# Graph attention on one core: five sums ahead of the last gather, the result between two one-hots

## The chip, the cores and the metric

The kernel runs on one core of a Trainium2 chip, in one launch. The metric is the device time of an execution in microseconds (us). The core's engines work side by side and meet at semaphores: PE (TensorE, matmuls into PSUM), DVE (VectorE), ACT (ScalarE), POOL (GpSimd) and SP, which here only issues DMAs. Each engine takes its own instructions strictly in the order in which the program gives them.

## The reference

A graph attention layer over 4096 nodes with 64 features, 50000 edges and 4 heads of 64 outputs.

```python
x_proj[h] = x @ weight[h]
for h in range(n_heads):
    src_att = np.sum(x_proj[h, src_nodes] * att_src[h], axis=-1)
    dst_att = np.sum(x_proj[h, dst_nodes] * att_dst[h], axis=-1)
    edge_scores[h] = src_att + dst_att
edge_scores = np.where(edge_scores > 0, edge_scores, 0.2 * edge_scores)
output[h, dst] = sum over its edges of exp(edge_scores[h, i]) * x_proj[h, src]
output[h, dst] /= sum over its edges of exp(edge_scores[h, i]) + 1e-8
```

The last two lines are written here as sums; the reference loops over edges and nodes. The output is node by node, the four heads side by side: 4096 x 256.

## The kernel before

Until about 104 us the edges are sorted: keyed by stretches of source nodes and blocks of destination nodes, sorted on DVE, written out and read back by their counts. Beside it PE computes the scores of all nodes. The result of this stage is, for each of 32 blocks of 128 destination nodes (`b`), a list of edges in 16 groups of 128 places (`NT` = 16), in DRAM (`bin_dram`).

Then a loop over the blocks (`Blocks.run`) does the layer itself. It is software-pipelined by hand: in the turn of block `b`, DVE and PE work on several blocks at once, and the order in which the Python code issues the instructions is the order on each engine. The steps of a turn:

- `load(b + 4)`: SP brings the list of a later block, the same for all partitions, into `bc` (1 MB, one of four buffers).
- `values(b)`: DVE multiplies the gathered features of block `b` by its weights, head by head, into `val`: one instruction over 16 groups x 4 heads x 64 features. The text calls it the product; its line is L641.
- `gather(b + 1, c)` for the three parts `CH` = 6, 6 and 4 groups: PE multiplies one-hot matrices `oh` by the features and scores of the nodes (`xa`, `adb`, L607 to L609) into a PSUM tile `ps` of three banks. There are two such tiles, taken in turn. ACT then takes exponentials of the scores, plain and times 0.2 (`ex`, L619), and copies the gathered one-hots and features into `xs` (L621).
- `project(b - 2)`: PE multiplies the transposed sums `aT` of an earlier block by the weight matrix into the lower half of `pt` (L784); it stands between the second and the third part of the gather.
- `give(b - 2)`: DVE divides that by the denominators (`inv`) into `res` (L794), one of two buffers, and SP stores it to the output (L798).
- `onehot(b + 2)`: DVE compares the list with the partition numbers: two instructions, L589 and L590, the second for the other half of the sources.
- `invert(b - 1)`: reciprocal of denominators, L791. Here some blocks also have one small step of the list `checks`, which counts whether any stretch of edges was too long.
- `weights(b + 1)`: DVE takes the maximum of the two exponentials, L632, into the places of `val` between the features; this makes the leaky ReLU.
- `sums(b)`: PE adds up the 16 groups in one PSUM bank, `acc` (L703), features and denominators together. After groups 9 and 12 it also transposes the two halves of the earlier block's sums into the upper half of `pt` (`turn(b - 1, ...)`, L774); after the second half ACT copies the transposes to `aT` (L779). At the end ACT takes the sums and denominators out of the bank (`take`, L764 and L766).

In one block, `told`, the first of the sums is followed by a matmul with one column that adds up the lengths' flag `long`, in the same bank behind the sums, and DVE compares it into `over` (L706, L707). If it is set, a branch after the loop does everything again in pieces; with these inputs it isn't taken.

The blocks 30 and 31 are computed in another way, with the product in three parts (`lastly`, `last`), and `finish` writes the last result. In three blocks POOL and DVE unpack another window of lists (`unpack`, after the sums).

`pt` is one PSUM bank, `acc` another, the two `ps` tiles take the other six.

Of the kernel before, what the change touches and what calls it, by code (L numbers as in the profile page):

```python
# [11 lines left out]
P = 128  # L12
ALPHA = 0.2
F32 = mybir.dt.float32
BF16 = mybir.dt.bfloat16
I32 = mybir.dt.int32
OP = mybir.AluOpType
# [33 lines left out]
def kernel(ctx: ExitStack, tc: tile.TileContext, x: bass.AP, edge_index: bass.AP,  # L51
# [4 lines left out]
    H, _, Dout = weight.shape  # L56
# [453 lines left out]
    NT = NR  # L510
# [21 lines left out]

    CH = ((0, 6), (6, 6), (12, 4))
    S0 = P + H
    XW = 208
    PW = 256

    class Blocks:
# [39 lines left out]

        def onehot(self, b, t0=0, nt=NT):
            if b >= ND:  # L580
                return
            narrow = self.narrow and b > 0
            if t0 == 0:
                self.oh[b] = self.narrow[b % 2] if narrow else (self.wp if self.narrow else self.bp).tile(
                    [P, 3 * NT * W2], BF16, name="oh")
            oh, bc = self.oh[b], self.bc[b]
            lo, hi = (LOW, HIGH) if narrow else (W2, 0)
            e = (2 * t0 * W2, [2 * W2, nt], [1, W2 + lo])
            V.tensor_scalar(out=av(oh[:], *e), in0=av(bc[:], *e), scalar1=pF[:, 0:1], scalar2=None, op0=OP.is_equal)  # L589
            V.tensor_scalar(out=av(oh[:], (2 * NT + t0) * W2 + hi, [W2, nt], [1, W2 - hi]),  # L590
                            in0=av(bc[:], (2 * t0 + 1) * W2 + hi, [2 * W2, nt], [1, W2 - hi]),
                            scalar1=pF[:, 1:2], scalar2=None, op0=OP.is_equal)

        def gather(self, b, c):

# [20 lines left out]
            for i in range(n):  # L616
                kinds[2](i, t0 + i, start=False, stop=True, skip_group_check=True)
            for k, scale in enumerate((1.0, ALPHA)):
                S.activation(out=av(ex[:], 2 * (k * H * NT + t0), [2, n], [2 * NT, H], [1, 2]),  # L619
                             in_=av(ps[:], P, [PW, n], [1, H], [0, 2]), func=ACTF.Exp, scale=scale)  # L620
# [73 lines left out]

        def sums(self, b, t0=0, n=NT, told=False, between={}):

# [5 lines left out]
            for t in range(t0, t0 + n):  # L702
                T.matmul(out=acc[:, 0:AW], lhsT=xs[:, t, 0:P], rhs=val[:, t, :], start=(t == 0), stop=(t == NT - 1),  # L703
                         **how)
                if t == 0 and told:
                    T.matmul(out=acc[0:1, AW:AW + 1], lhsT=long[:], rhs=ones[:], start=False, stop=True, **how)  # L706
                    V.tensor_scalar(out=over[:], in0=acc[0:1, AW:AW + 1], scalar1=0.5, scalar2=None, op0=OP.is_gt)  # L707
                if t in between:
# [11 lines left out]
        def run(self, first=0, also={}, checks=()):  # L720
# [3 lines left out]
            for b in range(first, ND):  # L724
# [5 lines left out]
                if b not in self.full:  # L730
                    self.values(b)
                for c in range(len(CH)):
                    if c == 2:
                        self.sink.project(b - 2)
                    self.gather(b + 1, c)
                self.sink.give(b - 2)
                self.onehot(b + 2)
                if checks:
                    checks.pop(0)()
                self.sink.invert(b - 1)  # L740
                if apart:
                    self.lastly(b + 1, 0)
                else:
                    self.weights(b + 1)
                self.sums(b, told=b == told, between={9: lambda: self.sink.turn(b - 1, 0), 12: lambda: self.sink.turn(b - 1, 1)})
                if apart:
# [5 lines left out]
    class Finish:  # L752
# [48 lines left out]
        def give(self, b):  # L801
            if b not in self.aT:
                return
            self.aT.pop(b)
            res = self.fp.tile([P, H, Dout], F32, name="res")
            self.scaled(b, res, self.pt[:, 0:C], 0, H)
# [12 lines left out]
        def finish(self, b, to, wait):  # L819
            self.invert(b)  # L820
            res = self.fp.tile([P, H, Dout], F32, name="res")
            for k, t in enumerate(self.aT.pop(b)):
# [230 lines left out]
```

## Time and profile before

| | us |
|---|---|
| median of three runs (277.97 to 278.76) | 278.16 |
| the profiled execution | 278.39 |
| its span, first to last instruction | 276.5 |
| busy in the span: DVE | 246.2 (89%) |
| PE matmuls | 208.8 (75%) |
| PE weight loads | 181.3 (66%) |
| ACT | 202.8 (73%) |
| POOL | 44.4 (16%) |

The span includes the sort, in which DVE is busy and PE mostly not; in the loop over the blocks, 124 to 265 us, DVE, PE and ACT are all busy over nine tenths of the time. The shares alone don't tell which of the three sets the time there: that is read from one block in the timeline, by who stands still, for whom, and for how long. A row of the timeline gives the start, the duration, and in brackets the time for which the engine stood idle just before, with the instruction that released it. Instructions of one engine overlap at their ends, so a step's cost is the distance between starts, not its duration.

### The profile page before, as it was taken

Reading aid. Unit: us, or ns where it says so; the run is one execution under the profiler, and the core shown is the slowest. Engines: PE = TensorE matmul, PEld = TensorE weight load, DVE = VectorE, ACT = ScalarE, POOL = GpSimd, SP = SyncE. Lnnn points to the kernel's source line nnn. Section 1 sums busy time; section 2 is a strip of 40 time slices with the busy share of each in tenths; the row PEclk is TensorE's granted clock in tenths of the full one; section 3 lists DMA queues with packets and bytes.
Section 4 is the critical chain, followed back from the end, with each engine's and each line's share of the span. In section 5 each row is a group of like instructions: output and inputs, shape, how many; then the busy total and the mean of one; then the engine's idle time right before and its main releaser. Section 6 shows DMA issues by size and latency. Waiting matters only on the chain. (4 is left out here: it accounts for less than half of the span.)

```text
span 276.5 us, 6793 instructions
## 1 busy us (share of the span) xinstructions
PE 208.8 (75%) x2551; PEld 181.3 (66%) x2551; DVE 246.2 (89%) x657; ACT 202.8 (73%) x516; POOL 44.4 (16%) x84
## 2 busy tenths in 40 slices
PE   0002769996001998979999999988999999999994
PEld 0002559996001454768888888977888888888883
DVE  4999999919999998889999999997999999998972
ACT  3980650006999929798989898897898989989871
POOL 7898600041000004203030020000000000000000
PEclk9999985555555699999999999999999999999998
DMA  3008000010000001795949558855866757572101
GB/s 116 1 0 163 10 2 2 0 57 19 1 0 0 2 0 47 190 411 165 398 115 385 206 188 342 287 210 193 264 232 233 261 216 293 210 247 111 41 21 63
DMA packets 13190, 39.43 MB, mean 143 GB/s; under 512 B 2208, under 2 KB 8416, under 8 KB 9568
## 3 DMA queue, kind: packets, MB, share of 16 engines
q1 hardware_dynamic: 10752, 36.84, 36.9%
q10 hardware_dynamic: 1696, 1.51, 2.4%
q0 software_dynamic: 704, 0.59, 0.9%
q8 instruction: 21, 0.34, 0.5%
q14 instruction: 17, 0.14, 0.2%
HBM read 33.96 MB, written 4.98 MB: 141 GB/s over the span
## 5 line engine op out<-in xcount | busy, mean ns | idle before, releaser
L621 ACT CAST xs<-ps 128x1176 bf16<-128x1176 f32 (+1 forms) x96 | 103.1, 1076 | 0.0
L641 DVE TENSOR_TENSOR val<-xs,val 128x4096 bf16<-128x4096 bf16 (+2 forms) x35 | 71.7, 2048 | 3.3
L703 PE MATMUL acc<-val,xs 128*128 128x264 bf16 x496 | 67.9, 276 | 1.4 <-DVE over L707 1.3
L607 PE MATMUL ps<-xa,oh 128*128 128x68 bf16 x512 | 51.8, 193 | 9.3 <-ACT xs L621 8.8
L703 PEld LDWEIGHTS <-xs 128*128 128x128 bf16 x496 | 46.5, 98 | 6.8 <-issue 1.5
L608 PEld LDWEIGHTS <-oh 128*128 128x128 bf16 x512 | 40.8, 97 | 15.2 <-issue 15.0
L608 PE MATMUL ps<-adb,oh 128*128 128x132 bf16 x512 | 49.5, 221 | 0.0
L607 PEld LDWEIGHTS <-oh 128*128 128x128 bf16 x512 | 43.9, 98 | 1.0 <-DVE oh L589 0.3
L619 ACT ACTIVATE ex<-ps 128x48 bf16<-128x48 f32 (+1 forms) x192 | 32.8, 243 | 6.7 <-PE ps L608 6.1
L589 DVE TENSOR_SCALAR oh<-bc,pF 128x3328 bf16<-128x3328 bf16 (+4 forms) x38 | 36.0, 948 | 1.8 <-ACT bc L577 1.1
L609 PE MATMUL ps<-xa,oh 128*128 128x68 bf16 x512 | 36.3, 194 | 0.3 <-DVE oh L590 0.3
L609 PEld LDWEIGHTS <-oh 128*128 128x128 bf16 x512 | 28.7, 97 | 0.9 <-DVE oh L590 0.5
L506 PEld LDWEIGHTS scores<-uv,xT 64*128 64x128 f32 x128 | 27.4, 328 | 0.2 <-issue 0.2
L506 PE MATMUL scores<-uv,xT 64*128 64x4 f32 x128 | 27.4, 351 | 0.0
L332 ACT ACTIVATE junk<-kr,nb 128x512 f32<-128x512 f32 x32 | 23.1, 722 | 1.1
L248 DVE TENSOR_TENSOR sB<-sA 128x128 f32<-128x128 f32 (+6 forms) x90 | 22.7, 305 | 0.1
L590 DVE TENSOR_SCALAR oh<-bc,pF 128x1664 bf16<-128x1664 bf16 (+4 forms) x38 | 22.1, 582 | 0.0
L248 DVE TENSOR_TENSOR sZ<-sB 128x128 f32<-128x128 f32 (+7 forms) x87 | 21.7, 302 | 0.1
L794 DVE TENSOR_TENSOR res<-pt,inv 128x256 f32<-128x256 f32 x31 | 13.1, 424 | 9.5 <-PE pt L784 7.5
L784 PE MATMUL pt<-Wbd,aT 128*128 128x128 f32 x124 | 21.4, 295 | 0.1
L779 ACT COPY aT<-pt 128x256 f32<-128x256 f32 x31 | 11.5, 373 | 10.8 <-PE pt L774 10.8
L342 PE MATMUL cnt_ps<-sgn,sel 128*128 128x17 f32 (+1 forms) x10 | 2.2, 349 | 22.9 <-POOL attbd L475 22.9
(173 smaller groups left out, 294.4 us busy)
## 6 DMA issues: line engine op xcount, KB each, us to landing
bc<-gat_bins SPq DMA_DIRECT2D x28, 1024.0 KB, 5.9
out_dram<-res SPq DMA_DIRECT2D x32, 128.0 KB, 2.4
bc<-gat_bins SPq DMA_DIRECT2D x4, 384.0 KB, 4.6
bc<-gat_bins SPq DMA_DIRECT2D x2, 256.0 KB, 5.7
eD<-in_edge_index_dram ACTq DMA_DIRECT2D x2, 195.0 KB, 3.5
eS<-in_edge_index_dram SPq DMA_DIRECT2D x2, 195.0 KB, 3.5
gat_sorted<-sY SPq DMA_DIRECT2D x1, 256.0 KB, 2.0
gat_sorted<-ki SPq DMA_DIRECT2D x1, 256.0 KB, 2.0
```

What stands on the lines that cost most here:

```text
L248: V.tensor_tensor(out=out, in0=in0, in1=in1, op=op)
L332: todo = [lambda b=b: S.activation(out=junk[:], in_=v, func=ACTF.Sign, bias=nbnd[:, b:b + 1], scale=1.0, accum_out=sgn[:, b:b + 1]) for b ...
L506: T.matmul(out=scores[:, k * NB + b, :], lhsT=nodes(b), rhs=uv[:, k, :], start=(k == 0 and b == 0), stop=True, skip_group_check=True)
L589: V.tensor_scalar(out=av(oh[:], *e), in0=av(bc[:], *e), scalar1=pF[:, 0:1], scalar2=None, op0=OP.is_equal)
L590: V.tensor_scalar(out=av(oh[:], (2 * NT + t0) * W2 + hi, [W2, nt], [1, W2 - hi]), in0=av(bc[:], (2 * t0 + 1) * W2 + hi, [2 * W2, nt], [1, ...
L607: kinds = [lambda i, t, **how: T.matmul(out=ps[:, i, P:P + XC], lhsT=hot(2 * t + 1), rhs=xa[:, 2 * t, :], **how), lambda i, t, **how: T.ma ...
L608: lambda i, t, **how: T.matmul(out=ps[:, i, 0:S0], lhsT=hot(2 * t), rhs=adb[:, b, :], **how),
L609: lambda i, t, **how: T.matmul(out=ps[:, i, P:P + XC], lhsT=hot(2 * NT + t), rhs=xa[:, 2 * t + 1, :], **how)]
L619: S.activation(out=av(ex[:], 2 * (k * H * NT + t0), [2, n], [2 * NT, H], [1, 2]), in_=av(ps[:], P, [PW, n], [1, H], [0, 2]), func=ACTF.Exp ...
L621: S.copy(out=xs[:, t0:t0 + n, 0:P + XC], in_=ps[:, 0:n, 0:P + XC])
L641: V.tensor_tensor(out=av(val, t0 * AW, [VW, H * n], [1, Din]), in0=av(xs, S0 + t0 * XW, [XW, n], [0, H], [1, Din]), in1=av(val, t0 * AW + ...
L703: T.matmul(out=acc[:, 0:AW], lhsT=xs[:, t, 0:P], rhs=val[:, t, :], start=(t == 0), stop=(t == NT - 1), **how)
```

## The change

- The turn's order on PE: the projection and the first five of the 16 sums (`AHEAD` = 5) now come between the second and the third part of the gather; the other eleven sums follow the third part. The two transposes of the earlier block's sums stand after groups 11 and 13 instead of 9 and 12.
- `values(b)` is issued as two instructions, for the first 12 groups and the last 4.
- The result `res` (`give`) is issued between the two one-hot instructions instead of ahead of them.
- `res` has three buffers instead of two.
- The flag's matmul goes behind the third part of the gather, into the third bank of its `ps` tile, of which that part uses two, and the comparison follows it there.

```diff
@@ -531,6 +531,7 @@
             nc.sync.dma_start(out=bin_dram[8 * i:8 * i + 8].rearrange("b g k e -> (b g) k e"), in_=tb)
 
     CH = ((0, 6), (6, 6), (12, 4))
+    AHEAD = 5
     S0 = P + H
     XW = 208
     PW = 256
@@ -576,8 +577,9 @@
                          stop=True, skip_group_check=True)
             copy(out=self.bc[b][:, t0 * PW:(t0 + n) * PW], in_=av(ps[:], 0, [1, n * PW]))
 
-        def onehot(self, b, t0=0, nt=NT):
+        def onehot(self, b, t0=0, nt=NT, between=lambda: None):
             if b >= ND:
+                between()
                 return
             narrow = self.narrow and b > 0
             if t0 == 0:
@@ -587,11 +589,12 @@
             lo, hi = (LOW, HIGH) if narrow else (W2, 0)
             e = (2 * t0 * W2, [2 * W2, nt], [1, W2 + lo])
             V.tensor_scalar(out=av(oh[:], *e), in0=av(bc[:], *e), scalar1=pF[:, 0:1], scalar2=None, op0=OP.is_equal)
+            between()
             V.tensor_scalar(out=av(oh[:], (2 * NT + t0) * W2 + hi, [W2, nt], [1, W2 - hi]),
                             in0=av(bc[:], (2 * t0 + 1) * W2 + hi, [2 * W2, nt], [1, W2 - hi]),
                             scalar1=pF[:, 1:2], scalar2=None, op0=OP.is_equal)
 
-        def gather(self, b, c):
+        def gather(self, b, c, told=False):
 
 
             if b >= ND:
@@ -615,6 +618,10 @@
                     kinds[k](i, t0 + i, start=(i % 2 == 0 and k == 0), stop=False, skip_group_check=True)
             for i in range(n):
                 kinds[2](i, t0 + i, start=False, stop=True, skip_group_check=True)
+            if told:
+                assert n % 2 == 0 and n < CH[0][1]
+                T.matmul(out=ps[0:1, n, 0:1], lhsT=long[:], rhs=ones[:], start=True, stop=True)
+                V.tensor_scalar(out=over[:], in0=ps[0:1, n, 0:1], scalar1=0.5, scalar2=None, op0=OP.is_gt)
             for k, scale in enumerate((1.0, ALPHA)):
                 S.activation(out=av(ex[:], 2 * (k * H * NT + t0), [2, n], [2 * NT, H], [1, 2]),
                              in_=av(ps[:], P, [PW, n], [1, H], [0, 2]), func=ACTF.Exp, scale=scale)
@@ -692,7 +699,7 @@
             self.sink.give(b - 1)
             self.sink.finish(b, [t[:, 2, 0:P] for t in ps], self.psa.tile([P, L], F32, name="wait", tag="acc")[:])
 
-        def sums(self, b, t0=0, n=NT, told=False, between={}):
+        def sums(self, b, t0=0, n=NT, between={}):
 
             xs, val = self.xs[b], self.val[b]
             if t0 == 0:
@@ -702,9 +709,6 @@
             for t in range(t0, t0 + n):
                 T.matmul(out=acc[:, 0:AW], lhsT=xs[:, t, 0:P], rhs=val[:, t, :], start=(t == 0), stop=(t == NT - 1),
                          **how)
-                if t == 0 and told:
-                    T.matmul(out=acc[0:1, AW:AW + 1], lhsT=long[:], rhs=ones[:], start=False, stop=True, **how)
-                    V.tensor_scalar(out=over[:], in0=acc[0:1, AW:AW + 1], scalar1=0.5, scalar2=None, op0=OP.is_gt)
                 if t in between:
                     between[t]()
             if t0 + n == NT:
@@ -728,21 +732,22 @@
                     continue
                 self.load(b + 4, CH if self.sink.apart and b == ND // 2 else ((0, NT),))
                 if b not in self.full:
-                    self.values(b)
-                for c in range(len(CH)):
-                    if c == 2:
-                        self.sink.project(b - 2)
+                    for t0, n in ((0, CH[2][0]), CH[2]):
+                        self.values(b, t0, n)
+                for c in range(2):
                     self.gather(b + 1, c)
-                self.sink.give(b - 2)
-                self.onehot(b + 2)
+                self.sink.project(b - 2)
+                self.onehot(b + 2, between=lambda: self.sink.give(b - 2))
                 if checks:
                     checks.pop(0)()
                 self.sink.invert(b - 1)
+                self.sums(b, 0, AHEAD)
+                self.gather(b + 1, 2, told=b == told)
                 if apart:
                     self.lastly(b + 1, 0)
                 else:
                     self.weights(b + 1)
-                self.sums(b, told=b == told, between={9: lambda: self.sink.turn(b - 1, 0), 12: lambda: self.sink.turn(b - 1, 1)})
+                self.sums(b, AHEAD, NT - AHEAD, between={11: lambda: self.sink.turn(b - 1, 0), 13: lambda: self.sink.turn(b - 1, 1)})
                 if apart:
                     self.lastly(b + 1, 1)
                 if b in also:
@@ -802,7 +807,7 @@
             if b not in self.aT:
                 return
             self.aT.pop(b)
-            res = self.fp.tile([P, H, Dout], F32, name="res")
+            res = self.fp.tile([P, H, Dout], F32, name="res", bufs=3)
             self.scaled(b, res, self.pt[:, 0:C], 0, H)
             self.store(b, res)
 
@@ -818,7 +823,7 @@
 
         def finish(self, b, to, wait):
             self.invert(b)
-            res = self.fp.tile([P, H, Dout], F32, name="res")
+            res = self.fp.tile([P, H, Dout], F32, name="res", bufs=3)
             for k, t in enumerate(self.aT.pop(b)):
                 T.matmul(out=to[k], lhsT=t, rhs=Wbd[:, k, :], start=True, stop=True, skip_group_check=True)
                 self.scaled(b, res, to[k], k * H // 2, H // 2)
```

On DVE, in the block's turn from the maximum over `ex` on: `val` are weights and values, `oh` the one-hots, `pt` the projected sums. Before:

```order
L632 TENSOR_TENSOR val<-ex 128x4x16x2 [waits Activation_49]
L641 TENSOR_TENSOR val<-xs,val 128x64x64 [waits DVE_49,Activation_49]
L794 TENSOR_TENSOR res<-pt,inv 128x256 [waits DMAHW7_49,PE_49,Activation_49]
L589 TENSOR_SCALAR oh_218<-bc,pF 128x16x208 [waits DMAHW6_49]
L590 TENSOR_SCALAR oh_218<-bc,pF 128x16x104
L791 RECIPROCAL inv<-den 128x4 [waits Activation_49]
```

The same turn after the change:

```order
L639 TENSOR_TENSOR val<-ex 128x4x16x2 [waits Activation_49]
L648 TENSOR_TENSOR val<-xs,val 128x48x64 [waits DVE_49]
L648 TENSOR_TENSOR val<-xs,val 128x16x64 [waits Activation_49]
L591 TENSOR_SCALAR oh_218<-bc,pF 128x16x208 [waits DMAHW6_49,PE_49]
L799 TENSOR_TENSOR res<-pt,inv 128x256 [waits DMAHW5_49,PE_49,Activation_49]
L593 TENSOR_SCALAR oh_218<-bc,pF 128x16x104
L796 RECIPROCAL inv<-den 128x4 [waits Activation_49]
```

The product is two instructions, and only the second waits for ACT; the result has moved behind the first one-hot.

On PE, from the projection to the first transpose, where `ps` is a gather's PSUM tile and `acc` the sums' bank; rows left out repeat the kinds beside them. Before:

```order
L784 MATMUL pt<-Wbd,aT 128x128 [waits Activation_49]
...
L607 LDWEIGHTS oh_217 [waits PE_49]
L607 MATMUL ps<-xa,oh_217 128x68 [waits Activation_49]
...
L703 LDWEIGHTS xs
L703 MATMUL acc<-val,xs 128x264 [waits DVE_49]
...
L774 MATMUL pt<-ident,sum 128x128 [waits DVE_49]
```

The same stretch after the change:

```order
L789 MATMUL pt<-Wbd,aT 128x128 [waits Activation_49]
...
L710 LDWEIGHTS xs [waits DVE_49,PE_49]
L710 MATMUL acc<-val,xs 128x264 [waits Activation_49]
...
L610 LDWEIGHTS oh_217 [waits PE_49]
L610 MATMUL ps<-xa,oh_217 128x68 [waits Activation_49]
...
L779 MATMUL pt<-ident,sum 128x128 [waits DVE_49]
```

Five sums stand ahead of the gather's third part, and the wait for DVE's values stands ahead of both; seven more sums stand between the third part and the first transpose.

## Rows read from the trace of the kernel before

**Rows 1.** Timeline of DVE, one block: start us, us, engine, line, instruction [idle before].
```profile
198.60 2.29 DVE L641 TENSOR_TENSOR val<-xs,val 128x4096 bf16<-128x4096 bf16 x1
201.14 0.42 DVE L794 TENSOR_TENSOR res<-pt,inv 128x256 f32<-128x256 f32 x1 [0.25 <-PE pt L784]
201.48 1.08 DVE L589 TENSOR_SCALAR oh<-bc,pF 128x3328 bf16<-128x3328 bf16 x1
202.47 0.65 DVE L590 TENSOR_SCALAR oh<-bc,pF 128x1664 bf16<-128x1664 bf16 x1
203.04 0.17 DVE L791 RECIPROCAL inv<-den 128x4 f32<-128x4 f32 x1
203.12 0.25 DVE L632 TENSOR_TENSOR val<-ex 128x128 bf16<-128x128 bf16 x1
203.48 2.29 DVE L641 TENSOR_TENSOR val<-xs,val 128x4096 bf16<-128x4096 bf16 x1
```

**Rows 2.** Timeline of PE over the same block.
```profile
198.92 0.19 PE L607 MATMUL ps<-xa,oh 128*128 128x68 bf16 x1
...
200.36 0.69 PE L784 MATMUL pt<-Wbd,aT 128*128 128x128 f32 x4
...
201.30 0.19 PE L607 MATMUL ps<-xa,oh 128*128 128x68 bf16 x1 [0.25 <-ACT xs L621]
...
201.77 1.29 PE L703 MATMUL acc<-val,xs 128*128 128x264 bf16 x10
...
203.79 0.19 PE L607 MATMUL ps<-xa,oh 128*128 128x68 bf16 x1
```

**Rows 3.** Timeline of ACT over the same block.
```profile
199.91 0.31 ACT L619 ACTIVATE ex<-ps 128x48 bf16<-128x48 f32 x2 [0.19 <-PE ps L608]
...
202.34 0.36 ACT L619 ACTIVATE ex<-ps 128x32 bf16<-128x32 f32 x2
...
203.66 0.37 ACT L779 COPY aT<-pt 128x256 f32<-128x256 f32 x1 [0.26 <-PE pt L774]
```

**Rows 4.** Timeline of DVE near the loop's start.
```profile
124.64 2.28 DVE L641 TENSOR_TENSOR val<-xs,val 128x4096 bf16<-128x4096 bf16 x1
126.84 0.42 DVE L794 TENSOR_TENSOR res<-pt,inv 128x256 f32<-128x256 f32 x1
...
131.44 0.42 DVE L794 TENSOR_TENSOR res<-pt,inv 128x256 f32<-128x256 f32 x1
```

**Rows 5.** Groups by line and shape, 110 to 260 us: busy us, mean ns.
```profile
L641 DVE TENSOR_TENSOR val<-xs,val 128x4096 bf16<-128x4096 bf16 x28 | 64.2, 2292 | 2.6
...
L641 DVE TENSOR_TENSOR val<-xs,val 128x1536 bf16<-128x1536 bf16 x3 | 2.9, 959 | 0.3
...
L641 DVE TENSOR_TENSOR val<-xs,val 128x1024 bf16<-128x1024 bf16 x2 | 1.4, 692 | 0.2
```

**Rows 6.** Timeline of DVE, a block with a check and an unpacking.
```profile
137.99 0.15 DVE L411 TENSOR_TENSOR over_d<-we,ws 128x4 f32<-128x4 f32 x1
...
138.85 2.28 DVE L641 TENSOR_TENSOR val<-xs,val 128x4096 bf16<-128x4096 bf16 x1
```

**Rows 7.** Timeline of PE, block in which the flag is told.
```profile
187.26 1.17 PE L703 MATMUL acc<-val,xs 128*128 128x264 bf16 x9 [1.28 <-DVE over L707]
```

**Rows 8.** Timeline of DVE at the end.
```profile
261.99 2.29 DVE L641 TENSOR_TENSOR val<-xs,val 128x4096 bf16<-128x4096 bf16 x1
...
272.21 0.49 DVE L794 TENSOR_TENSOR res<-ps,inv 128x128 f32<-128x128 f32 x2 [0.81 <-DMA out_dram<-res]
```

**Rows 9.** Timeline of PE at the end.
```profile
264.66 0.19 PE L607 MATMUL ps<-xa,oh 128*128 128x68 bf16 x1 [0.25 <-ACT xs L621]
...
267.44 0.71 PE L784 MATMUL pt<-Wbd,aT 128*128 128x128 f32 x4
267.99 0.83 PE L681 MATMUL ps<-xs,val 128*128 128x128 bf16 x12
```

**Rows 10.** DMA issues by line: KB each, median us to landing.
```profile
bc<-gat_bins SPq DMA_DIRECT2D x28, 1024.0 KB, 5.9
```

## The prediction

> **What bounds the kernel now.** I read the profiled execution by engine in time, first DVE, then PE, then ACT, over one block of the loop. On DVE [rows 1] the product of one block starts at 198.60 and that of the next at 203.48, so a block takes 4.88 us. Between them DVE stands still once: the result `res` starts at 201.14, idle 0.25 us until PE's projection `pt`. Where DVE doesn't wait, the result starts 2.20 us after the product, 0.08 before the product's own end [rows 4]. Here it starts 2.54 after, so 0.34 us of the block is lost and DVE's own work is 4.88 - 0.34 = 4.54 us. Near the loop's start, where DVE waits for nobody, two results lie 4.60 us apart, with one small check of 0.07 between them [rows 4]: 4.53, the same.
>
> Why the projection is late stands on PE [rows 2]. Gather parts one and two take 198.92 to 200.36 (1.44 us), then comes the projection, then the third part, which is held until 201.30 by ACT's copy `xs` of the first part: three parts share two PSUM buffers, and the third takes that of the first. The third part takes 0.47 (to 201.77), sixteen sums and two transposes 2.02 (to 203.79), and the next block begins. The projection in front of another matmul takes 267.99 - 267.44 = 0.55 [rows 9]. So PE's work is 1.44 + 0.55 + 0.47 + 2.02 = 4.48 us of 4.87, and 0.39 is the wait for ACT. First part, ACT's copy, third part, sums, first part: this ring sets 4.87, and DVE's wait for `pt` is its echo. Taking out PE's wait therefore leaves DVE as the slowest engine, at 4.54.
>
> **Five sums ahead of the third part.** PE goes from the projection to five sums (18 sums and transposes in 2.02 are 0.11 each, so 0.56), and reaches the third part 1.44 + 0.55 + 0.56 = 2.55 after the block's first gather. The copy that frees its buffer lets it go 201.30 - 198.92 = 2.38 after it. The wait is covered, with 0.17 to spare. What comes later: the third part ends at 2.55 + 0.47 = 3.02, and 0.27 later ACT could start its exponentials (those of the first part start at 199.91 [rows 3], its gathers end half of 1.44 after 198.92); but ACT is busy with the second part until 3.42 (202.34 [rows 3]), as before, so `ex` of the third part isn't delayed. DVE's maximum over `ex` needs it at 3.42 + 0.36 + 0.06 = 3.84.
>
> **Values in two pieces.** The sums may start on the first twelve groups. The line through the shapes of the product [rows 5] is (2292 - 959) / (4096 - 1536) = 0.52 ns per element; the piece of 3072 elements takes 959 + 1536 x 0.52 = 1759 ns, that of 1024 takes 692 [rows 5]: 2451 against 2292, 0.16 more. An instruction starts 0.08 before its forerunner's end [rows 4], so one more instruction costs 0.16 - 0.08 = 0.08 net, and this is on DVE, the new bound. No row has the two pieces behind each other: the cost lies between 0, if the first piece starts sooner because it no longer needs the third copy, and 0.16. I take 0.08. The section "The TRN2 errata" of the Trainium skill's page "VectorE: DVE Perf Modes" says that an operation on SBUF pays a fixed latency each time, so that many small tiles pay it per tile, and measured about 150 cycles at 0.96 GHz: 0.16 us, the very intercept of rows 5. By that rule alone the split would cost the full 0.16 a block, which speaks against the change; the 0.08 of overlap in rows 4 speaks against the rule's full price.
>
> **Result between the one-hots.** It costs DVE nothing in length. The result no longer has to be ready at once: it is asked for 2.28 + 0.99 (201.48 to 202.47) = 3.27 us after the product's start. Count from there for the block in which DVE never waits (4.62): the second one-hot ends at 3.27 + 0.34 + 0.65 = 4.26. The first piece ends at 1.76, so with 0.08 of hand-over PE's five sums start at 1.84, the third part ends at 2.87, seven more sums at 3.66. Then PE's first transpose, which writes into the same `pt` as the result is read from, waits for the result's end at 3.27 + 0.42 + 0.08 = 3.77: a new wait of 0.11. From there four sums and two transposes (0.67) lead to the next first gather at 4.44, behind the one-hot at 4.26. The next projection ends at 4.44 + 1.44 + 0.69 = 6.57, and the result of that block wants it at 4.62 + 3.27 = 7.89: 1.3 to spare. The maximum over the third part's `ex` is due at 4.44 + 3.84 = 8.28 and starts at 4.62 + 4.26 = 8.88: 0.6 to spare. So DVE waits for nobody and PE absorbs its 0.14 of slack in its two waits. On SP's queue the store of a result, and behind it the load four blocks ahead, go out 1 us later in the block; a load lands in 5.9 us [rows 10] and is used two to three blocks (over 9 us) later: nothing.
>
> **Flag's matmul, third result buffer.** The one-time 1.28 us in which PE waits until DVE has read the flag out of the sums' bank [rows 7] goes; it is inside the stretch that the sum replaces. The last result waits 0.81 for a store of the result two before [rows 8]; with three buffers that goes. It is worth between 0 and 0.81, since PE's last products are near; I take 0.4.
>
> **The sum.** From the second block's product at 124.64 [rows 4] to that of block 30 at 261.99 [rows 8] are 28 blocks and 137.35 us. After: 28 x (4.54 + 0.08) = 129.36. Added work of DVE in it: the unpacking of a window and a check, 0.86 from the check to the product [rows 6] where the block without them has 0.44 from the reciprocal [rows 1], so 0.42, of which 0.07 is the check's (0.15 less the overlap). Two unpackings are 0.70, seven checks 0.49, the flag's comparison 0.07: 1.26. Together 130.6, a gain of 6.7. At the end the projection of block 29 stands at 267.44, 5.45 after the last full product. Before, it came 2.78 after the third part's start at 264.66 [rows 9]: 0.47, 13 sums and one transpose (1.57), and 0.74 for the second transpose and its copy. After: the product's first piece 1.84, sums and third part 1.03, nine sums and a transpose 1.12, the same 0.74 (0.37 of it the copy [rows 3]): 4.73, a gain of 0.7. With the 0.4: 7.8. The profiled execution took 278.39 us, 276.5 of it span; it is 0.23 over the median of the runs, so it stands for them. 278.4 - 7.8 = 270.6.
>
> **Rivals.**
> The split costs its whole intercept: 28 x 0.08 = 2.2 more, 272.8. For it: the intercept in rows 5. Against: every DVE pair in rows 1 overlaps unless the second needs the first's output, and the two pieces don't need each other.
> PE becomes the bound: it now stops for the first piece, for the result and for the second one-hot, and if each stop costs 0.09 from release to first row (the projection's end 201.05 to `res` 201.14 [rows 1, 2]) that nothing hides, PE's block is 4.48 + 0.27 = 4.75, so 28 x 0.13 = 3.6 more, 274.2. Against: two of the stops vanish as soon as PE is the later one.
> Slower than before: the change closes a ring over three engines and two blocks: result and hand-over (0.50), PE's second transpose three instructions later (0.34) and the way to ACT's copy of it (0.74 - 0.37), that copy and those of sums and denominators (203.66 to the next first `ex` at 199.91 + 4.88, less 0.19 idle [rows 3]: 0.94), the evictions up to the third part's `ex` (2.43 + 0.42), DVE's maximum, product and one-hot (0.36 + 2.28 + 0.99): 8.63 us, 4.32 a block. It decides from 2 x 4.62 = 9.24, 0.6 more. To be slower than now a block must take some 4.93, 1.23 more in the ring, 0.14 at each of its nine hand-overs: 28 x 0.31 = 8.7 over the forecast, 279.3, and DVE would wait at the maximum over `ex`. Against: the hand-overs are in the rows already.
> The change doing less than it says: most of DVE's 0.34 stays as a wait at another instruction; with 0.28 of it kept, 28 x 0.28 = 7.8, the gain is eaten: 278.4.
>
> **How the numbers follow.** Forecast 0.70; split in full 0.12; PE the bound 0.10; ring 0.05; gain eaten 0.03. About 0.3% (0.8 us) is what a measurement can tell from no change: faster 0.92, same 0.03, slower 0.05. The time is 270.6. The range goes down to 269.2, with half a free split (28 x 0.04 = 1.1) and some of the last wait, and up to 273.8, past the full split and most of the way to PE as the bound.
>
> **What would show it.** Blocks 4.62 apart on DVE with no idle time before the result; products of 1.76 and 0.69 us; PE's third part without a wait for `xs`, and small waits, some 0.14 a block, at the first sum and at the first transpose; no 1.28 behind the flag; no wait for a store in the last result. I am wrong if DVE idles before the maximum over `ex`, or if the two pieces start more than 1.75 apart.

## The result, and the profile after

The changed kernel takes 269.27 us, median of 4 runs (268.50 to 269.91), beside 278.07 (277.88 to 278.76) for the kernel before in the same comparison: a ratio of 0.9678, 95% interval 0.9647 to 0.9709. It is 3.2% faster. The forecast was 270.6, so the direction was right and the size of the gain nearly, but the time fell 1.3 us under the forecast, to the very foot of the range (269.2); two of the four runs lie below it. Two terms of the sum were off, in opposite directions, and the experiments show that one part of the change, the split of the product, does something else than the prediction said of it.

| | before, us | after, us |
|---|---|---|
| the profiled execution | 278.39 | 269.41 |
| its span | 276.5 | 267.5 |
| busy: DVE | 246.2 (89%) | 246.9 (92%) |
| PE matmuls | 208.8 (75%) | 207.3 (78%) |
| ACT | 202.8 (73%) | 200.2 (75%) |
| product of block 2 to product of block 30 | 137.35 | 129.41 |

DVE does as much as before and in less time: the gain is idle time gone. One block on DVE, to be laid beside [rows 1] (timeline: start us, us, engine, line, instruction; the two pieces of the product stand in one row, x2):

```profile
199.33 0.25 DVE L639 TENSOR_TENSOR val<-ex 128x128 bf16<-128x128 bf16 x1
199.61 2.36 DVE L648 TENSOR_TENSOR val<-xs,val 128x3072 bf16<-128x3072 bf16 x2
201.89 1.08 DVE L591 TENSOR_SCALAR oh<-bc,pF 128x3328 bf16<-128x3328 bf16 x1
202.88 0.42 DVE L799 TENSOR_TENSOR res<-pt,inv 128x256 f32<-128x256 f32 x1
203.22 0.65 DVE L593 TENSOR_SCALAR oh<-bc,pF 128x1664 bf16<-128x1664 bf16 x1
203.78 0.17 DVE L796 RECIPROCAL inv<-den 128x4 f32<-128x4 f32 x1
203.86 0.24 DVE L639 TENSOR_TENSOR val<-ex 128x128 bf16<-128x128 bf16 x1
204.14 1.76 DVE L648 TENSOR_TENSOR val<-xs,val 128x3072 bf16<-128x3072 bf16 x1
```

A block takes 204.14 - 199.61 = 4.53 us instead of 4.88, and no row has idle time. Two intervals are to be compared with those of before. From the product's start to the next instruction it is 2.28 (199.61 to 201.89), where one undivided product took 2.20 [rows 4]: the split costs the 0.08 that was foreseen. But from the maximum to the product it is 0.28 (199.33 to 199.61), where it was 0.36 (203.12 to 203.48 in [rows 1]): 0.08 comes back that was not foreseen.

The same stretch on PE, to be laid beside [rows 2]:

```profile
195.01 0.19 PE L610 MATMUL ps<-xa,oh 128*128 128x68 bf16 x1
...
196.45 0.69 PE L789 MATMUL pt<-Wbd,aT 128*128 128x128 f32 x4
196.98 0.73 PE L710 MATMUL acc<-val,xs 128*128 128x264 bf16 x5
197.54 0.19 PE L610 MATMUL ps<-xa,oh 128*128 128x68 bf16 x1
...
198.82 0.33 PE L779 MATMUL pt<-ident,sum 128*128 128x128 f32 x1
...
199.54 0.19 PE L610 MATMUL ps<-xa,oh 128*128 128x68 bf16 x1
```

The five sums follow the projection at once, the third part starts at 197.54 with no wait for ACT, and PE comes round in 4.53 us too. The waits of DVE and PE over the loop and the tail, first of the kernel before, then of the changed one (engine, line, what it waited for: us in total, times, longest):

```profile
PE ps L607 <- ACT xs L621: 7.4, 29, 0.4
...
DVE res L794 <- PE pt L784: 7.5, 23, 1.8
```

```profile
PE acc L710 <- ACT xs L628: 0.6, 2, 0.3
...
DVE res L799 <- ACT aT L784: 1.0, 1, 1.0
DVE res L799 <- PE pt L789: 0.8, 1, 0.8
```

The pair that set the loop, PE for `xs` and DVE for `pt`, is gone (7.4 us in 29 waits, 7.5 in 23), and so is the wait of the last result for a store [rows 8]. What is left on DVE is in the tail, apart from one block of the loop. That is the block in which the flag is told, here on DVE and then on ACT:

```profile
185.23 0.11 DVE L624 TENSOR_SCALAR over<-ps 1x1 int32<-1x1 f32 x1
185.69 0.28 DVE L639 TENSOR_TENSOR val<-ex 128x128 bf16<-128x128 bf16 x1 [0.35 <-ACT ex L626]
186.01 2.36 DVE L648 TENSOR_TENSOR val<-xs,val 128x3072 bf16<-128x3072 bf16 x2
```

```profile
185.38 0.29 ACT L626 ACTIVATE ex<-ps 128x32 bf16<-128x32 f32 x2 [0.88 <-DVE over L624]
```

The 1.28 on PE [rows 7] is gone. But the flag now lies in the same tile `ps` as the scores, if in another bank, and its comparison comes ahead of the exponentials in the program: ACT's exponentials wait 0.88 for DVE's comparison, and DVE's maximum waits 0.35 for ACT. The block takes 5.04, 0.50 more than its neighbours. DVE idle ahead of this maximum is what the prediction named as a sign of being wrong; it is there in this one block of the 28.

### The profile page after: what moved, and what is told of

Its sections match the earlier page's. It is cut to its first block, busy times and chain, and to the rows that moved or that the text cites. A ratio compares the mean times of both kernels' runs of the same rounds, so it can differ in the third digit from the quotient of the medians.

```text
span 267.5 us, 6825 instructions
## 1 busy us (share of the span) xinstructions
PE 207.3 (78%) x2551; PEld 179.8 (67%) x2551; DVE 246.9 (92%) x686; ACT 200.2 (75%) x516; POOL 42.6 (16%) x84
## 3 DMA queue, kind: packets, MB, share of 16 engines
HBM read 33.96 MB, written 4.98 MB: 146 GB/s over the span
## 4 chain that ended last, share of the span: by engine, by line
PE 46%; DVE 38%; DMA 7%; ACT 3%; issue 3%; POOL 1%; SPq 1%; ACTq 0%; DVEq 0%; POOLq 0%
PE acc L710 18%; PE ps L611 9%; DVE sB L248 7%; DVE sZ L248 7%; DVE sA L248 7%; PE pt L789 5%; PE ps L612 5%; PE ps L610 5%; DVE sY L248 4%; PE pt L779 3%; DMA bc<-gat_bins 3%; DVE val L648 3%; DVE oh L591 2%; DMA eD<-in_edge_index_dram 1%; POOL raw L431 1%
## 5 line engine op out<-in xcount | busy, mean ns | idle before, releaser
L648 DVE TENSOR_TENSOR val<-xs,val 128x3072 bf16<-128x3072 bf16 (+2 forms) x64 | 74.3, 1198 | 1.5
L710 PE MATMUL acc<-val,xs 128*128 128x264 bf16 x496 | 74.0, 276 | 1.2 <-ACT xs L628 0.6
L710 PEld LDWEIGHTS <-xs 128*128 128x128 bf16 x496 | 45.8, 100 | 6.8 <-PE pt L789 1.8
L439 ACT ACTIVATE kr<-raw,goff 128x256 f32<-128x256 f32 x2 | 1.0, 507 | 24.0 <-DMA raw<-gat_sorted,wi 24.0
L779 PE MATMUL pt<-ident,sum 128*128 128x128 f32 x62 | 18.2, 297 | 0.2
```

The lines of the kernel that those rows point to most:

```text
L648: V.tensor_tensor(out=av(val, t0 * AW, [VW, H * n], [1, Din]), in0=av(xs, S0 + t0 * XW, [XW, n], [0, H], [1, Din]), in1=av(val, t0 * AW + ...
L779: T.transpose(out=self.pt[:, C + k * P:C + (k + 1) * P], in_=self.sum[b][:, k * P:(k + 1) * P], identity=ident[:])
```

## The experiments

Each starts from the changed kernel or, where it says so, from the kernel before; the two whose headings end in "too" add their edit to the experiment ahead of them. The ratios are to the kernel before.

### One product instead of two pieces

```diff
-                    for t0, n in ((0, CH[2][0]), CH[2]):
-                        self.values(b, t0, n)
+                    self.values(b)
```

> The kernel after the change, with the values of a block in one instruction again. Theory (DVE sets the block; two pieces are 0.08 us longer, but the first starts 0.08 sooner after the maximum, since it waits for one semaphore instead of two): the product starts 0.36 after the maximum instead of 0.28 and takes 2.20 instead of 2.28, so blocks stay 4.53 to 4.55 apart; the 0.19 that the unpacking costs in three blocks goes; 268.5 to 269.5. Rival 1 (the second piece is a net cost of 0.08, as predicted): 267.0. Rival 2 (PE needs the early piece: sums start 0.45 later, and the maximum over the third part's exponentials waits): blocks of 4.65 or more, 272.5 or more.

Measured: 273.86 us (273.27 to 274.74), ratio 0.9844, 0.9819 to 0.9869: 4.6 us slower than with the pieces. The theory falls. Its second rival had the time (272.5 or more), but the wait is at the product and not at the maximum. DVE's rows over one block, with ACT's third part and PE's sums between them:

```profile
201.14 2.29 DVE L648 TENSOR_TENSOR val<-xs,val 128x4096 bf16<-128x4096 bf16 x1 [0.27 <-ACT xs L628]
...
205.88 2.29 DVE L648 TENSOR_TENSOR val<-xs,val 128x4096 bf16<-128x4096 bf16 x1 [0.31 <-ACT xs L628]
```

```profile
203.58 0.72 PE L710 MATMUL acc<-val,xs 128*128 128x264 bf16 x5
204.13 0.19 PE L610 MATMUL ps<-xa,oh 128*128 128x68 bf16 x1
```

```profile
204.81 0.33 ACT L626 ACTIVATE ex<-ps 128x32 bf16<-128x32 f32 x2
204.98 0.86 ACT L628 CAST xs<-ps 128x784 bf16<-128x784 f32 x1
```

There is a ring of its own, through one block. The product ends at 203.43, the five sums start at 203.58, the third part behind them at 204.13, ACT's exponentials at 204.81, its copy ends at 205.84, and the next product, which reads that copy, starts at 205.88: 4.74 us (the blocks take 4.74 and 4.70 in turn). DVE waits for `xs` 23 times, 6.5 us together. With sums ahead of the third part the undivided product stands at both ends of this ring, and the pieces open it at both: the sums start after the first piece, and only the second piece reads the third copy.

### The small piece first

```diff
-                    for t0, n in ((0, CH[2][0]), CH[2]):
+                    for t0, n in (CH[2], (0, CH[2][0])):
```

> The kernel after the change, with the piece of 4 groups ahead of the piece of 12. Theory: the first piece now waits for DVE and for ACT's copy, two semaphores, so it starts 0.36 after the maximum again, and the 0.08 that the second instruction costs stands uncovered: blocks of 4.62, 28 x 0.085 = 2.4 more, 271.6. Rival (the shorter gap comes with the piece's size, or there is no gap to lose): 269.3.

Measured: 275.65 us (275.57 to 275.79), ratio 0.9907, 0.9883 to 0.9930. Neither size was right. The blocks take 4.77 (202.46 to 207.23):

```profile
202.46 2.36 DVE L648 TENSOR_TENSOR val<-xs,val 128x1024 bf16<-128x1024 bf16 x2 [0.27 <-ACT xs L628]
...
207.23 2.36 DVE L648 TENSOR_TENSOR val<-xs,val 128x1024 bf16<-128x1024 bf16 x2 [0.26 <-ACT xs L628]
```

It is the ring of the last experiment, longer by the split: the piece that reads the third copy comes first, and the groups that the first sums need come last. So it isn't the division that helps but which groups stand first.

### The third part ahead of the sums again

```diff
-                self.sums(b, 0, AHEAD)
                 self.gather(b + 1, 2, told=b == told)
                 ...
+                self.sums(b, 0, AHEAD)
```

> The kernel after the change, with the gather's third part ahead of all 16 sums again; pieces, result between the one-hots, flag and buffers as after. Theory (PE's wait for ACT's copy of the first part sets 4.87): blocks of 4.87 again once DVE's lead is used up, PE idle 0.25 ahead of the third part, DVE waiting at the maximum or the result; 276 to 278. Rival (the later place of the result alone takes DVE's wait away): 270.

Measured: 276.89 us (276.28 to 277.31), ratio 0.9948, 0.9933 to 0.9964. Blocks are 4.87 (196.86 to 201.73), as before the change. The waits of the whole execution:

```profile
PE ps L610 <- ACT xs L628: 8.8, 32, 0.6
...
DVE val L639 <- ACT ex L626: 4.6, 20, 0.4
```

PE's wait for the copy of the first part is back, and DVE, whose result no longer needs `pt` early, loses its time at the maximum instead, 0.23 a block. So the sums ahead are what opens the ring that the prediction named.

### The result ahead of both one-hots again

```diff
-                self.onehot(b + 2, between=lambda: self.sink.give(b - 2))
+                self.sink.give(b - 2)
+                self.onehot(b + 2)
```

> The kernel after the change, with the result ahead of both one-hots again. Theory (five sums ahead are enough): the projection ends some 2.1 us after the product's start and the result asks for it at 2.2, so blocks stay at 4.53 to 4.55, 269.0 to 269.8. Rival (the place of the result is needed): DVE idles ahead of the result again, 0.1 to 0.3 a block, 272 to 277.

Measured: 269.13 us (268.81 to 269.49), ratio 0.9667, 0.9644 to 0.9690: no difference from the changed kernel. The result starts 2.28 after the product's first piece and doesn't wait:

```profile
199.88 2.36 DVE L648 TENSOR_TENSOR val<-xs,val 128x3072 bf16<-128x3072 bf16 x2
202.16 0.42 DVE L800 TENSOR_TENSOR res<-pt,inv 128x256 f32<-128x256 f32 x1
```

Beside the split product the place of the result is worth nothing: once PE has lost its wait, the projection is early enough for either place.

### The sums ahead alone

The kernel before with the five sums moved ahead of the third part and nothing else; the two transposes stay after groups 9 and 12:

```diff
-                for c in range(len(CH)):
-                    if c == 2:
-                        self.sink.project(b - 2)
+                for c in range(2):
                     self.gather(b + 1, c)
+                self.sink.project(b - 2)
                 ...
+                self.sums(b, 0, 5, told=b == told)
+                self.gather(b + 1, 2)
                 self.weights(b + 1)
-                self.sums(b, told=b == told, between=...)
+                self.sums(b, 5, NT - 5, between=...)
```

> The kernel before with five sums ahead of the third part and nothing else: values in one instruction, the result ahead of both one-hots, the flag's matmul in the sums' bank, two result buffers. Theory (one undivided product closes a ring: product, five sums, third part, ACT's exponentials and copy, next product): blocks of 4.70 to 4.74 as in the run with one piece, the flag's wait of some 1.28 still there where the changed kernel loses 0.50, the last result late by 0.4: 273.9 + 0.8 + 0.4 = 275.1 us (274.3 to 275.9), most of DVE's idle time in front of the product, behind ACT's copy of xs. Rival (the sums ahead alone are what the change is worth, since they are what takes PE's wait for ACT away): blocks of 4.54, 270 to 271 us.

Measured: 276.99 us (275.93 to 278.43), ratio 0.9962, 0.9940 to 0.9984: slower than expected by 1.9, and far from the rival. Most blocks are 4.70 to 4.80, a little over the theory's 4.70 to 4.74, but the wait that the theory named is mostly not there. DVE waits more often and longer for the projection than for the copy:

```profile
DVE res L795 <- PE pt L785: 2.8, 13, 0.8
...
DVE val L641 <- ACT xs L621: 1.3, 5, 0.4
```

The copy is close behind: it ends at 202.88 and 207.63, and the products start at 202.97 and 207.67. But what holds most blocks is a second ring that the undivided product closes, over two blocks: the product ends at 195.76, the five sums start at 195.91, the projection behind the other sums and two parts of the next gather stands at 199.85, the result, ahead of both one-hots here, starts at 200.63, and the next product at 202.97, 9.50 after that first one's start (193.47). So the sums do wait for the undivided product here too, 13 times and 4.0 us together, and where this leaves DVE waiting seems to depend on the place of the result; no run changes that alone beside an undivided product.

The block with the flag was under-estimated as well:

```profile
187.98 0.28 DVE L632 TENSOR_TENSOR val<-ex 128x128 bf16<-128x128 bf16 x1 [1.50 <-ACT ex L619]
188.68 2.29 DVE L641 TENSOR_TENSOR val<-xs,val 128x4096 bf16<-128x4096 bf16 x1 [0.43 <-ACT xs L621]
```

```profile
186.54 0.61 PE L703 MATMUL acc<-val,xs 128*128 128x264 bf16 x4 [1.78 <-DVE over L707]
```

With the flag in the sums' bank and sums ahead, PE stops for 1.78 with the third part still behind it, and DVE's maximum for 1.50; the block takes 6.75. With the flag in its own bank, in the run with one piece, it was 5.36 (181.64 to 187.00). The two runs differ in more than the flag, so the 1.4 us between them is only an estimate of what the flag's own bank is worth with sums ahead.

### Two result buffers

```diff
-            res = self.fp.tile([P, H, Dout], F32, name="res", bufs=3)
+            res = self.fp.tile([P, H, Dout], F32, name="res")
```

> The changed kernel with two result buffers instead of three. Theory (the last result waits for the store of the result two before it): the last result is held by that store, 0.3 to 0.8 us of wait, 269.6 to 269.9 us, the loop unchanged at 4.53 to 4.54 a block. Rival (the last products are the later ones either way): 269.2 to 269.4, no wait for a store.

Measured: 269.54 us (269.52 to 269.78), ratio 0.9690, 0.9667 to 0.9712. The loop is unchanged, and the last result waits as in [rows 8]:

```profile
263.44 0.49 DVE L799 TENSOR_TENSOR res<-ps,inv 128x128 f32<-128x128 f32 x2 [0.81 <-DMA out_dram<-res]
```

From the last full product to the end of the last result it is 10.06 (253.87 to 263.93) against 9.61 in the changed kernel (254.01 to 263.62): 0.45 in the trace. The times alone, 0.27 apart, can't tell it from nothing.

### The pieces alone

The kernel before with the product in two pieces and nothing else:

```diff
-                    self.values(b)
+                    for t0, n in ((0, CH[2][0]), CH[2]):
+                        self.values(b, t0, n)
```

> The kernel before with the values in two pieces and nothing else. Theory (an undivided product waits for two engines, DVE's maximum and ACT's last copy xs, and its second semaphore is an instruction of its own, 32 of them in the trace of before; the first piece waits for the maximum alone): the first piece starts 0.28 after the maximum instead of 0.36, the two pieces take 2.36 instead of 2.29, so DVE's own work stays 4.54, with 6 instead of 32 such instructions; the block is set by PE and ACT as before, 4.87, and the time is 278.0 to 278.6 us, no difference from before. Rival 1 (0.28 comes from the sums ahead, not from the split): the piece starts 0.35 or 0.36 after the maximum, DVE's own work is 4.61 or 4.62. Rival 2 (the split alone lets the sums start earlier): blocks under 4.85 and 277.5 us or less.

Measured: 278.19 us (277.89 to 278.82), ratio 1.0000, 0.9986 to 1.0014. The theory holds in each point. First a block of its DVE, then its instructions on the product's line:

```profile
198.01 0.24 DVE L632 TENSOR_TENSOR val<-ex 128x128 bf16<-128x128 bf16 x1
198.28 2.36 DVE L641 TENSOR_TENSOR val<-xs,val 128x3072 bf16<-128x3072 bf16 x2
200.90 0.42 DVE L795 TENSOR_TENSOR res<-pt,inv 128x256 f32<-128x256 f32 x1 [0.25 <-issue]
```

```profile
L641 DVEq EVENT_SEMAPHORE  x6: 21/21/21, 108.0 to 120.8; - x6
```

And the row of the kernel before, for the same line:

```profile
L641 DVEq EVENT_SEMAPHORE  x32: 21/21/21, 108.2 to 261.9; - x32
```

An undivided product waits for two engines, the maximum of DVE and the last copy of ACT, and a wait instruction stands ahead of it in the queue. The first piece has no such instruction, and it starts 0.27 to 0.28 after the maximum instead of 0.35 to 0.36. It isn't the copy itself that is late: these are DVE and ACT near the loop's start in the kernel before.

```profile
128.88 0.24 DVE L632 TENSOR_TENSOR val<-ex 128x128 bf16<-128x128 bf16 x1
129.23 2.29 DVE L641 TENSOR_TENSOR val<-xs,val 128x4096 bf16<-128x4096 bf16 x1
```

```profile
127.42 0.89 ACT L621 CAST xs<-ps 128x784 bf16<-128x784 f32 x1
```

The product starts 0.35 after its maximum here too, although the copy had ended at 128.31, 0.92 us earlier. Nor is it the size of the piece: in the changed kernel the small pieces ahead of the loop's first whole product, which have a wait instruction each (the six at this line again), start as late after the end of their maximum as the undivided product does. A piece of 1024 elements starts at 120.74, 0.11 after its maximum's end (120.45 + 0.18), with its copy over since 119.59; the undivided product starts 0.11 after (128.88 + 0.24 to 129.23), the first piece without a wait instruction 0.03 after (198.01 + 0.24 to 198.28). So the split takes 0.08 and gives 0.08, and on DVE it is free. Whether it is the wait instruction or the second wait that costs the 0.08 is not told apart; they go together. And as PE and ACT set the block here, the free split changes nothing.

### The reciprocal between the maximum and the product

```diff
-                self.sink.invert(b - 1)
                 self.sums(b, 0, AHEAD)
                 ...
                     self.weights(b + 1)
+                self.sink.invert(b - 1)
```

> The changed kernel with DVE's reciprocal moved from ahead of the maximum to between the maximum and the first piece. Theory (DVE's own work sets the block, and the 0.28 between the maximum's start and the first piece's is a wait for the maximum's own output, under which another instruction fits): the 0.08 that the reciprocal takes goes away, blocks of 4.46 to 4.49, where PE's own work of 4.48 becomes the next bound: 269.3 - 28 x 0.06 = 267.6 us (267.0 to 268.3). Rival 1 (the 0.28 is what each new instruction in that place costs, whoever stands ahead): the product starts 0.28 after the reciprocal, blocks 4.53, 269.0 to 269.6. Rival 2 (PE is bound as well, its hand-overs not hidden): blocks 4.52 or more although DVE idles, 269 to 270.

Measured: 267.32 us (266.99 to 267.40), ratio 0.9602, 0.9579 to 0.9624: 1.95 us faster than the changed kernel, as the theory said (267.6). The blocks take 4.46 (198.50 to 202.96):

```profile
202.66 0.27 DVE L639 TENSOR_TENSOR val<-ex 128x128 bf16<-128x128 bf16 x1
202.80 0.17 DVE L796 RECIPROCAL inv<-den 128x4 f32<-128x4 f32 x1
202.96 2.36 DVE L648 TENSOR_TENSOR val<-xs,val 128x3072 bf16<-128x3072 bf16 x2
```

From the maximum to the product it is 0.30 with an instruction in between, 0.28 without. So most of the 0.28 is a wait for the maximum's own output, and DVE's own work sets the block: 0.07 less of it is 0.07 less a block. In the two blocks of the loop with an unpacking, where other instructions fill that gap already, it gains only 0.01 (5.02 and 4.95 instead of 5.03 and 4.96). From the product of block 2 to that of block 30 it is 127.68 (124.42 to 252.10) instead of 129.41, 1.73 less; the rest of the 1.95 lies outside this stretch. PE, at 4.53 a block in the changed kernel, follows down to 4.46 and wasn't the bound.

### The flag's comparison behind the maximum, too

```diff
-                V.tensor_scalar(out=over[:], in0=ps[0:1, n, 0:1], ...)
+                self.flag = ps[0:1, n, 0:1]
                 ...
                     self.weights(b + 1)
+                if b == told:
+                    V.tensor_scalar(out=over[:], in0=self.flag, ...)
```

> The kernel with the reciprocal moved, and besides it DVE's comparison of the flag behind the maximum instead of ahead of ACT's exponentials over the same PSUM tile. Theory (the long block of 5.04 comes from ACT's exponentials, which wait for DVE's comparison because both read one tile, and the maximum waits for them): that block falls to 4.55 to 4.65, 0.4 less than the run with the reciprocal moved: 267.2 us (266.6 to 267.9). Rival (the block is long because of the comparison and its matmul themselves): still 4.9 to 5.1, no difference between the two.

Measured: 266.95 us (266.39 to 267.25), ratio 0.9590, 0.9566 to 0.9614. The told block takes 4.67 (179.95 to 184.62) instead of 4.98 with the reciprocal moved alone:

```profile
184.12 0.27 DVE L639 TENSOR_TENSOR val<-ex 128x128 bf16<-128x128 bf16 x1
184.46 0.15 DVE L750 TENSOR_SCALAR over<-ps 1x1 int32<-1x1 f32 x1
...
184.62 2.32 DVE L648 TENSOR_TENSOR val<-xs,val 128x3072 bf16<-128x3072 bf16 x2
```

The block is 0.02 over the range expected, and the maximum no longer waits for ACT. The trace shows the 0.3; the two times, 0.37 apart, have overlapping intervals.

### The unpacking's cast on ACT, too

```diff
-            (G if i else V).tensor_copy(out=tb, in_=t)
+            S.copy(out=tb, in_=t) if i else V.tensor_copy(out=tb, in_=t)
```

> The kernel with the reciprocal and the flag's comparison moved, and besides them the cast of a window's unpacking (tb, in the two of three windows that POOL casts) on ACT instead of POOL. Theory (in those blocks DVE's second piece and POOL's cast keep each other off: the piece takes 0.88 instead of 0.68, and starts late behind the cast): the two pieces take 2.36 there instead of 2.55, 0.2 less a block with a cast, 0.4 to 0.6 in all: 266.4 us (266.0 to 267.0). Rival (ACT has no room for the cast and gives the maximum's ex later): DVE waits in front of the maximum in those blocks, 266.9 to 267.6.

Measured: 266.62 us (266.35 to 266.81), ratio 0.9584, 0.9570 to 0.9598. The first two rows are DVE and POOL in a block with an unpacking in the changed kernel, the third is DVE in this one:

```profile
139.04 2.55 DVE L648 TENSOR_TENSOR val<-xs,val 128x3072 bf16<-128x3072 bf16 x2
...
139.19 1.86 POOL L530 CAST tb<-t 128x256 bf16<-128x256 int32 x1 [12.57 <-DVE t L529]
```

```profile
138.58 2.35 DVE L648 TENSOR_TENSOR val<-xs,val 128x3072 bf16<-128x3072 bf16 x2
```

There are three such casts, one more than the expectation says. With POOL's cast beside them the two pieces take 2.55 instead of 2.36, and with the cast on ACT 2.35. In the changed kernel the first piece ends 1.76 after its start, at 140.80, and POOL's cast ends 0.25 later, at 141.05. In the kernel before the cast took 2.39 to 2.40 us and so ended 0.26 to 0.27 after the one long product. It looks as if POOL came to its turn each time when a product had ended, and the second piece, where there is one, had to wait for POOL. The Trainium skill's page "SBUF — State Buffer", section "Who interferes with whom", says that a VectorE instruction with two inputs in SBUF contends with a GpSimd instruction that reads SBUF, and that the port pair they share is an exclusive lock. The rows agree: the cast ends 0.25 to 0.27 after the product's piece beside it, whether that takes 1.76 or 2.28. In time the 0.33 us between this run and the last are within their intervals; the trace shows 0.2 in each of the blocks.

This is the lowest time of the study, 1.0% below the changed kernel, though not told apart from the run before it.

## Where the prediction was right, and the step that failed

**What bounds the kernel: right.** The ring of first part, copy, third part and sums set 4.87, and DVE's own 4.54 came next. The third part put back ahead of the sums gives 4.87 again; and taking 0.07 from DVE's work takes 0.07 from the block.

**The split: the step that failed.** The prediction took 0.08 a block as its net cost, from bounds of 0 and 0.16, and named a reason for 0: the first piece no longer needs the third copy. That end was the true one; the time lay in the wait for a second engine, not in the copy, which was over. So the step that failed is the sum 4.54 + 0.08 = 4.62. The second piece did cost the 0.08, but the sum lacked the 0.08 that comes back at the first piece's start, and the net cost measured nothing: blocks of 4.53 to 4.54, so that 28 are 28 x 4.535 = 126.98 and not 129.36, 2.38 less. The rows for it stood in the trace of before: 32 wait instructions at the product's line, and 0.35 between maximum and product also where ACT's copy had long ended. The prediction looked at durations and overlaps, not at the wait instructions of the queue.

**What the loop holds beside the blocks: too small.** It was put at 1.26 us and measured 129.41 - 126.98 = 2.43. The flag's block was to cost 0.07 and cost 0.50, since the prediction counted the comparison's own time and took another bank for free of waits, though it is a bank of the tile that ACT reads. The collision with POOL's cast, 0.19 in each of three blocks, 0.57, was not foreseen at all. Of the other 0.17 most lies in the two unpackings. Their instructions stand between the maximum and the product, which are 0.70 apart there before and after (157.57 to 158.27, 157.09 to 157.79); without them the two were 0.35 apart before and are 0.28 now, so an unpacking costs 0.42 and not 0.35. That is the gap of the split again, not seen a second time. Together 1.17 more, which hid half of the first error: 2.38 - 1.17 = 1.21, the difference between forecast (130.6) and measured loop (129.41).

**The tail: right.** The projection of block 29, beside [rows 9]:

```profile
258.81 0.71 PE L789 MATMUL pt<-Wbd,aT 128*128 128x128 f32 x4 [0.24 <-ACT aT L784]
```

It stands 258.81 - 254.01 = 4.80 after the last full product, forecast 4.73, before 5.45. From there to the end of the last result it is 4.81 instead of 5.26, a gain of 0.45 where 0.4 was forecast, and with two buffers 0.45 is lost again. The 0.4 was a middle taken between 0 and 0.81, so that it came so near is luck. In all the traces show 7.94 + 0.65 + 0.45 = 9.04 where the forecast had 6.7 + 0.7 + 0.4 = 7.8.

**The waits on PE: nearly right.** The third part has no wait, as forecast. Of the small waits at the first sum and at the first transpose only the second shows, as a transpose of 0.33 instead of 0.27.

**The rivals.** The full price of the split, PE as the bound, the ring over three engines and a stall that stays are all refuted by blocks of 4.53 without idle time. None of them was the case that a part of the change is missing, and there the prediction's reading was thin: it costed the split as a burden that lets the sums start early, and never worked out what the block would be without it. It would be 4.72, as the run with one piece shows. The sums ahead alone bring 0.4% (276.99), the pieces alone nothing (278.19), the whole change, with both and the smaller edits, 3.2%. And the place of the result, to which the prediction gave a paragraph, is worth nothing beside the pieces. What the later place of the two transposes is worth, and whether five is the best number of sums, no run tells.

## What to carry to other kernels

When an order on one engine is changed to open a ring, look for the ring that the new order closes: here the moved sums tied the undivided product to later products, and only splitting it, with the early groups first, made the move pay. What an instruction costs is its distance from its neighbours, and this holds waits for the forerunner's output and for further semaphores: here an instruction that needs one engine less started 0.08 us earlier, and an independent one put into such a gap cost 0.02 instead of 0.08. A bank of its own didn't end the flag's wait here, since the bank was part of a tile that another engine was waiting to read.

## What the runs showed of the hardware that was not expected

- An instruction of DVE that reads its forerunner's output starts 0.28 us after the start of a maximum of 0.25, where an independent one starts 0.14 after it (202.66 to 202.80, the reciprocal moved). The Trainium skill's page "VectorE: DVE Perf Modes", section "The DRAIN you can't avoid", measured that a semaphore after each of eight copies costs nothing extra. No run here repeats that measurement; what is shown here is that a wait for the forerunner's output leaves a gap, and that filling it gained 0.07 us a block.
- The same instruction with a second engine to wait for starts 0.35 to 0.36 after the maximum, though the second engine is done: 0.07 to 0.08 more.
- POOL's cast of 128x256 took 1.86 or 2.40 us on POOL, according to the length of DVE's product beside it, and 0.41 on ACT.
